# Delta rule in a hybrid decoder step: 16x16 diagonal blocks of the inverse on VectorE, query-key products after it, and a seventh buffer for q, k, v and z

## The chip, the cores and the metric

The kernel runs on one core of one Trainium2 chip. TensorE (PE) multiplies matrices and loads its weights through a row of its own (PEld); VectorE (DVE), ScalarE (ACT) and GpSimd (POOL) work element by element; SyncE (SP) starts most of the DMAs. The metric is the device time of one execution in microseconds (us), lower is better. Several runs are given by their median. The trace is that of one profiled execution; times in it count from its first instruction.

## The reference

One inference step of a decoder with two layers, for a prompt of 256 tokens and for 8 samples of one token each, all in fp32. A layer has a mixer (four mLSTM heads and eight gated-delta heads behind one input projection `w_in`), cross attention over 256 memory tokens, and a SwiGLU. The change lies in the gated-delta heads of the prompt. Cut to these:

```python
def gdn_chunked(q, k, v, log_a, beta, S0):
    incl, strict = lower triangle with and without the diagonal
    def step(S, xs):                                   # one chunk of the sequence
        g = jnp.cumsum(gc, axis=1)
        decay_ts = jnp.exp(jnp.where(incl, g_t - g_s, -jnp.inf))
        A = jnp.where(strict, decay_ts * (k k^T) * beta, 0.0)
        rhs = vc - exp(g) * (kc @ S)
        U = triangular_solve(A, rhs, lower=True, unit_diagonal=True)
        wu = beta * U
        qk = (qc kc^T) * decay_ts
        o = exp(g) * (qc @ S) + qk @ wu
        S_new = exp(g_last) * S + (wend * kc)^T @ wu
        return S_new, o
```

What matters: per chunk and head a unit lower triangular system is solved, (I + A) U = rhs, and the products of q and k are needed only for the output `o`, after U is known.

## The kernel before

**Streams.** Nearly all matmul work is weights times activations. `stream` (L249) multiplies 2048 rows of a weight matrix by 264 columns (256 tokens and 8 samples). Weights arrive in blocks of 512 KB (`block`, L239): a DMA from SP brings `raw`, ACT copies it rounded as `wh`, DVE takes `wl` = `raw` - `wh`, and PE adds three products for each piece (high times high, high times low, low times high). `wh` and `wl` have three buffers each. ACT and DVE do this with raised priority.

**The order on PE.** PE's instructions are written out in the order in which the program issues them; the other engines' orders are made by the framework's planner, from priorities (program order, raised in some places) and its own estimates of when an operation can start. Small work that isn't a stream (decay, delta rule, samples, norms) is written as generators. `yield 2100.0` means: go on when the program's own clock, which counts estimated nanoseconds of PE work (`mm`, L67), is that much further. After each piece of a stream `pump` (L89) continues whatever is due. `finish` (L96) continues generators until given ones have ended, without streams between.

**The mixer stage** (`mixers`, L1091) goes through four pairs of delta heads. For each pair three streams make q, k and v, with a causal convolution of four taps on DVE (`gdn_inputs`, L831); from the second pair on a fourth stream makes z of the pair before (`gdn_z`, L852). q, k, v, z and the mLSTM's q, k and z come from one tag of buffers, "s", with `SB` = 6 of them (L553). After a pair's streams `gdn_prompt` (L594) is started for the 256 tokens, as two chunks of 128 for each of two heads, four matrices of 128x128 side by side (index i), and `gdn_sample` (L757) for the samples. A pair's `gdn_prompt` waits until that of the pair before has set `formed` (L738).

**`gdn_prompt`**, in the order of its visits to PE:

- transposes of k (`pkn`), then the products k k^T (`pk_`) and k q^T (`pq_`), four each, and on DVE the matrices N (k k^T scaled by the decay E and by beta) and W (k q^T times E) (L621 to L629);
- after 4500 of the clock the transposes of v (DVE makes `vn`), after 1600 those of q;
- the inverse begins: `Dm` starts as four identities; the level b = 1 is done on DVE with a mask `up[1]` (`u`, L648 to L651); `Dt` holds the transposes of Dm's 32x32 blocks;
- after 2700 the transposes of N (`pa`, copied by ACT to `A`, L653 to L656);
- the levels b = 2, 4, 8, 16, 32, 64 (L657 to L694) double the inverted diagonal blocks. Each has two visits: after 2100 the products `pp` of A and Dm, which DVE copies with a mask to `f`; after 1900 the products `pd` of Dt and f, which DVE subtracts from Dm. Up to b = 16 DVE then transposes Dm into Dt again;
- for each of the two chunks (L698 to L737): `pu` (inverse times right side), then `pS` (the new state, and W times the solution for the output), with the products `pr` of q and k with the state between the chunks.

At the end the outputs are normalised, and once z is there transposed (`oT`, L749), multiplied by z and split for the output projection. `finish(*gd[:4])` and `finish(*gd[4:])` (L1146, L1151) stand in front of the projection's two parts for these heads.

`copy` (L53) is ScalarE, `tt` and `stt` (L56, L59) are VectorE unless another engine is given. Rows of the profile carry these helpers' lines: L72 is `mm`, L76 `tr`, L54 `copy`, L57 `stt`, L60 `tt`.

Of the kernel before, what the change touches and what calls it, by code (L numbers as in the profile page):

```python
# [8 lines left out]
F32 = mybir.dt.float32  # L9
F32R = mybir.dt.float32r  # L10
AF = mybir.ActivationFunctionType
ALU = mybir.AluOpType
AX = mybir.AxisListType
PSUM = bass.MemoryType.PSUM

P = 128
D = 2048
# [9 lines left out]
XH = 4  # L27
MEM = 256
EPS = 1e-6
WB, VB, SB, NV = 10, 6, 6, 6  # L30
PRIO = 1000
Q0, K0, V0, O0 = 0, 512, 1024, 2048
IF0 = 3072
# [5 lines left out]
def bc(ap, axis, n):  # L39

    a = ap.unsqueeze(axis)
    shape = list(a.shape)
    shape[axis] = n
    return a.to_broadcast(shape)
# [3 lines left out]
def kernel(ctx: ExitStack, tc: tile.TileContext, io: dict, outs: list):  # L48
    nc = tc.nc
    (y_p, y_s, p_C, p_n, p_m, p_S, p_conv, p_k, p_v, s_C, s_n, s_m, s_S, s_conv) = outs  # L50
    act, dve, pool, pe = nc.scalar, nc.vector, nc.gpsimd, nc.tensor

    def copy(out, in_, scale=1.0):  # L53
        act.activation(out, in_, AF.Copy, scale=scale)  # L54

    def stt(out, a, s, b, o0, o1):  # L56
        dve.scalar_tensor_tensor(out=out, in0=a, scalar=s, in1=b, op0=o0, op1=o1)  # L57

    def tt(out, a, b, op, eng=None):  # L59
        (eng or dve).tensor_tensor(out=out, in0=a, in1=b, op=op)  # L60
# [6 lines left out]
    def mm(out, lhsT, rhs, start=True, stop=True):  # L67
        n = 1
        for x in rhs.shape[1:]:
            n *= x  # L70
        clock[0] += max(n, lhsT.shape[-1]) / 2.4 * (1 if rhs.dtype == F32R else 4)
        pe.matmul(out=out, lhsT=lhsT, rhs=rhs, start=start, stop=stop)  # L72
# [29 lines left out]
    cp = ctx.enter_context(tc.tile_pool(name="const", bufs=1))  # L102
# [7 lines left out]
    def ps(name):  # L110
        return pm.tile([P, 512], F32, name=name, tag="m")


    ident = cp.tile([P, P], F32, name="ident")
# [10 lines left out]
    def power(t, e):  # L125

        if len(t.shape) == 3:
            e = e[:t.shape[0], :t.shape[1] * t.shape[2]].rearrange("p (a b) -> p a b", a=t.shape[1])
        else:
            e = e[:t.shape[0], :t.shape[1]]  # L130
        tt(t, t, e, ALU.pow, pool)
# [7 lines left out]
                       channel_multiplier=1)  # L139

    up = {}
    b = 1
    while b < P:
        nb = P // (2 * b)
        m = cp.tile([P, nb], F32, name=f"up{b}")
        dve.memset(m, 1.0)
        pool.affine_select(out=m, in_=m, pattern=[[-2 * b, nb]], compare_op=ALU.is_ge, fill=0.0, base=0,
                           channel_multiplier=1)
        pool.affine_select(out=m, in_=m, pattern=[[2 * b, nb]], compare_op=ALU.is_ge, fill=0.0, base=b - 1,
                           channel_multiplier=-1)  # L150
        up[b] = m
        b *= 2

    twos = cp.tile([P, GH + MH], F32R, name="twos")
    dve.memset(twos.bitcast(F32), 0.0)
# [412 lines left out]
    def four(t):  # L568
        return t.rearrange("p (i t) -> p i t", i=4)

    def hc(t):
        return t.rearrange("p (h c) t -> p h c t", c=2)


    def gdn_decay(g, G, M, R):
# [15 lines left out]
        yield 2400.0  # L591
        R.E, R.eL = E, eL

    def gdn_prompt(l, g, s, G, M, R):  # L594
        h0 = 2 * g
        q, k, v = s

        def ch(t, i):
            return t[:, i // 2, (i % 2) * P:(i % 2 + 1) * P]
# [4 lines left out]
        E, eL = R.E, R.eL  # L604
# [13 lines left out]
        dve.tensor_scalar(out=kd, in0=kss, scalar1=0.25, scalar2=None, op0=ALU.mult)  # L618
        power(kd, hp)

        pk_, pq_ = ps("kk"), ps("kq")  # L621
        for i in range(4):
            mm(pk_[:, i * P:(i + 1) * P], ch(k, i), ch(k, i))
        for i in range(4):
            mm(pq_[:, i * P:(i + 1) * P], ch(k, i), ch(q, i))
        N, W = M.w("N"), M.w("W")
        for i in range(4):
            stt(N[:, i], pk_[:, i * P:(i + 1) * P], bs[:, i:i + 1], E[:, i], ALU.mult, ALU.mult)
        tt(W, four(pq_), E, ALU.mult)  # L629
        yield 4500.0  # L630
        pv = ps("vT")
        for i in range(4):
# [9 lines left out]
            act.activation(M.junk()[:, :P], pqn[:, i * P:(i + 1) * P], AF.Square, accum_out=qd[:, i:i + 1])  # L642
        dve.tensor_scalar(out=qd, in0=qd, scalar1=4.0 * EPS, scalar2=float(DK), op0=ALU.add, op1=ALU.mult)
        power(qd, hm)

        Dm, Dt, A = M.w("Dm"), M.w("Dt"), M.w("A")
        pool.tensor_copy(out=Dm, in_=bc(ident, 1, 4))
        u = M.v("u", (4, 64))  # L648
        tt(u, N[:, :, 1::2], bc(up[1], 1, 4), ALU.mult)
        tt(Dm[:, :, 1::2], Dm[:, :, 1::2], u, ALU.subtract)  # L650
        dve.transpose(Dt.rearrange("p i t -> p (i t)"), Dm.rearrange("p i t -> p (i t)"))  # L651
        yield 2700.0
        pa = ps("NT")  # L653
        for i in range(4):
            tr(pa[:, i * P:(i + 1) * P], N[:, i])
        copy(A, four(pa))  # L656
        b = 2  # L657
        while b < P:
            def halves(t, which, i=None):
                x = t.rearrange("p i t -> p (i t)") if i is None else t[:, i]  # L660
# [32 lines left out]
                dve.transpose(Dt[32:64, :, 0:32], Dm[0:32, :, 32:64])  # L693
            b *= 2  # L694

        o = M.w("o")
        S1 = None
        for c in range(2):  # L698
            yield 1600.0
            if c == 0:  # L700
                rhs = hc(vn)[:, :, 0]
            else:
                pr = ps("pr")
                for j in range(2):
                    mm(pr[:, j * P:(j + 1) * P], ch(k, 2 * j + 1), S1[:, j])
                for j in range(2):
                    mm(pr[:, T + j * P:T + (j + 1) * P], ch(q, 2 * j + 1), S1[:, j])
                rhs, qS = M.v("rhs"), M.v("qS")
                for j in range(2):
                    stt(rhs[:, j], pr[:, j * P:(j + 1) * P], G.en[:, h0 + j:h0 + j + 1], vn[:, 2 * j + 1], ALU.mult,  # L710
                        ALU.add)
                for j in range(2):
                    copy(qS[:, j], pr[:, T + j * P:T + (j + 1) * P], scale=G.eg[:, h0 + j:h0 + j + 1])
                yield 1800.0
            pu = ps("pu")
            for j in range(2):
                mm(pu[:, j * P:(j + 1) * P], Dm[:, 2 * j + c], rhs[:, j])
            w = M.v("wu")
            tt(w, pu[:, :T].rearrange("p (h t) -> p h t", h=2),
               bc(bs.rearrange("p (h c) -> p h c", c=2)[:, :, c], 2, P), ALU.mult)  # L720
            yield 1800.0
            pS_ = ps("pS")
            for j in range(2):
                mm(pS_[:, j * P:(j + 1) * P], kw[:, 2 * j + c], w[:, j])
            for j in range(2):
                mm(pS_[:, T + j * P:T + (j + 1) * P], W[:, 2 * j + c], w[:, j])
            Sn = M.v("S")
            po = pS_[:, T:].rearrange("p (h t) -> p h t", h=2)
            if c == 0:
                copy(Sn, pS_[:, :T].rearrange("p (h t) -> p h t", h=2))  # L730
                copy(hc(o)[:, :, 0], po)
            else:
                for j in range(2):
                    stt(Sn[:, j], S1[:, j], eL[:, j:j + 1], pS_[:, j * P:(j + 1) * P], ALU.mult, ALU.add)
                nc.sync.dma_start(out=p_S[l, 0, h0:h0 + 2].rearrange("h k v -> k h v"), in_=Sn)
                tt(hc(o)[:, :, 1], po, qS, ALU.add)
            S1 = Sn  # L737
# [14 lines left out]
        x = M.w("ox", (2, T))  # L752
# [338 lines left out]
    def mixers(l, nx, mx, st, nx2):  # L1091
# [26 lines left out]
        for g in range(4):  # L1118
            if g % 2 == 0:
                hs[g // 2] = hidden(f"gd{g}")  # L1120
            r = Run()
            r.z, r.E, r.at = None, None, 2 * (g % 2)
            r.formed, r.before = False, R[g - 1] if g else None
            r.hh, r.hl = hs[g // 2]
            R.append(r)
            S = st.tile([P, 2, NB, P], F32, name="S", tag="st")
            for j in range(2):
                nc.gpsimd.dma_start(out=S[:, j], in_=io["state_gdn_S"][l, :, 2 * g + j].rearrange("b k v -> k b v"))
            spawn(gdn_decay(g, G, M, r))
            if g == 0:  # L1130
                s = gdn_inputs(l, g, nx, cb, rawc, M, first)
            else:
                s = gdn_inputs(l, g, nx, cb, rawc, M)
            gd.append(spawn(gdn_prompt(l, g, s, G, M, r)))
            gd.append(spawn(gdn_sample(l, g, s, G, M, r, S, smp)))
            if g:
                gdn_z(l, g - 1, nx, M, R[g - 1])
# [315 lines left out]
    with tc.manual_schedule(engines={mybir.EngineType.PE}):  # L1453
# [25 lines left out]
        for c in range(3):  # L1479
            w = P if c < 2 else NB  # L1480
            mm(pr[:w, c:c + 1], nx.sa[0][:, c * P:c * P + w], ones[:, 0:1])
        for c in range(3):
            w = P if c < 2 else NB
# [3 lines left out]
        for q in range(4):  # L1487
            qs = slice(q * 512, (q + 1) * 512)
            for c in range(3):
                w = P if c < 2 else NB  # L1490
                o = nx.y[:w, c, qs]
                i = nx.pt[c][:w] if q == 3 else o
# [37 lines left out]
```

## Time and profile before

| what | value |
|---|---|
| median of 3 runs | 2990.75 us (2990.35 to 2992.3) |
| profiled execution | 2992.1 us, its span 2990.2 us |
| mean granted clock of PE | 0.997 |
| PE / DVE / ACT / POOL busy | 2929.9 / 2004.4 / 1466.8 / 496.4 us |
| instructions | 58126 |

The page gives busy times by engine, the span in 40 slices of 74.75 us with a digit for the tenths that each engine is busy, the chain of work that ended last, and groups of instructions by line, engine and operation. Other views give busy times in chosen windows, and the single instructions in order of time. Matmuls overlap in PE's pipeline, so their single durations add up to more than PE's busy time, which counts the time in which at least one is under way.

### The profile page before, as it was taken

The numbers are of one execution on the slowest core, as the hardware profiler recorded it, in microseconds if no ns is written. First come the engines' busy times: TensorE is split into PE (matmuls) and PEld (weight loads), VectorE is DVE, ScalarE is ACT, GpSimd is POOL, SyncE is SP. The second block draws the span as 40 slices with busy tenths as digits, with TensorE's granted clock in tenths as the row PEclk, the third lists the DMA queues.
The fourth block names the chain that finished last, engine by engine and source line by source line (L and its number), as shares of the span: only waits on it lengthen the run. The fifth ranks groups of instructions, "written<-read, shape, count | busy, mean of one in ns | idle before, by whom it ended". The sixth has DMA issues, their size and how long they took to land.

```text
span 2990.2 us, 58126 instructions
## 1 busy us (share of the span) xinstructions
PE 2929.9 (98%) x23475; PEld 2852.7 (95%) x23475; DVE 2004.4 (67%) x3365; ACT 1466.8 (49%) x2441; POOL 496.4 (17%) x660
## 2 busy tenths in 40 slices
PE   8999999999999999999999999999999999999998
PEld 7999999978999999999999999999699999999998
DVE  7888776877555555555688777678765555555555
ACT  6555455666433333333465555556564333334335
POOL 5222100352100000000231121003520000000001
PEclk9999999999999999999999999999999999999999
DMA  7555565666666666666655554756756666666664
GB/s 198 144 149 153 154 205 165 215 211 189 182 180 181 182 179 183 178 182 180 176 156 162 145 162 131 221 157 212 232 171 183 178 182 181 180 182 179 182 180 132
DMA packets 381251, 530.09 MB, mean 177 GB/s; under 512 B 25576, under 2 KB 226224, under 8 KB 380960
## 3 DMA queue, kind: packets, MB, share of 16 engines
q1 hardware_dynamic: 364328, 498.74, 56.2%
q0 software_dynamic: 7424, 25.20, 2.8%
q10 hardware_dynamic: 9232, 2.45, 0.4%
q8 instruction: 184, 3.01, 0.4%
q14 instruction: 83, 0.68, 0.1%
HBM read 502.88 MB, written 23.83 MB: 176 GB/s over the span
## 4 chain that ended last, share of the span: by engine, by line
PE 85%; DVE 8%; ACT 3%; issue 2%; DMA 1%; POOL 0%; SPq 0%; POOLq 0%; DVEq 0%; ACTq 0%
PE acc L72 75%; DVE wl L60 2%; PE kv L72 2%; DVE xl L57 1%; PE pd L72 1%; PE pp L72 1%; ACT wh L54 1%; DVE y L57 1%; DMA memn<-in_mem_prompt_dram 1%; PE dks L72 1%; PE sqC L72 0%; PE dS L72 0%; DVE xT L60 0%; PE accg L72 0%; DVE p L1325 0%
## 5 line engine op out<-in xcount | busy, mean ns | idle before, releaser
L60 DVE TENSOR_TENSOR wl<-raw,wh 128x1024 fp32r<-128x1024 f32 x880 | 1090.8, 1240 | 797.7 <-ACT wh L54 795.9
L54 ACT ACTIVATE wh<-raw 128x1024 fp32r<-128x1024 f32 x880 | 931.1, 1058 | 1242.2 <-PE acc L72 1130.1
L72 PE MATMUL acc<-xh,wh 128*128 128x264 f32 x4736 | 1367.6, 289 | 5.7 <-ACT wh L54 3.4
L72 PE MATMUL acc<-xh,wl 128*128 128x264 f32 x4736 | 1348.7, 285 | 0.9 <-DVE wl L60 0.7
L72 PE MATMUL acc<-xl,wh 128*128 128x264 f32 x4736 | 1347.5, 285 | 1.7 <-DVE xl L57 1.7
L72 PEld LDWEIGHTS acc<-xh,wh 128*128 128x128 f32 x4736 | 894.6, 189 | 10.5 <-issue 3.6
L72 PEld LDWEIGHTS acc<-xl,wh 128*128 128x128 f32 x4736 | 895.6, 189 | 4.7 <-DVE xl L57 2.3
L72 PEld LDWEIGHTS acc<-xh,wl 128*128 128x128 f32 x4736 | 893.9, 189 | 2.3 <-DVE wl L60 2.3
L72 PE MATMUL acc<-ffh,wh 128*128 128x264 f32 x1408 | 400.8, 285 | 0.6 <-DVE xT L60 0.5
L72 PE MATMUL acc<-ffl,wh 128*128 128x264 f32 x1408 | 400.8, 285 | 0.0
L72 PE MATMUL acc<-ffh,wl 128*128 128x264 f32 x1408 | 400.3, 284 | 0.0
L60 POOL TENSOR_TENSOR fg<-fg,rstd 128x264 f32<-128x264 f32 x88 | 95.3, 1112 | 1306.0 <-ACT fg L1412 1306.0
L72 PEld LDWEIGHTS acc<-ffh,wh 128*128 128x128 f32 x1408 | 264.8, 188 | 1.0 <-issue 1.0
L72 PEld LDWEIGHTS acc<-ffl,wh 128*128 128x128 f32 x1408 | 265.3, 188 | 0.0
L72 PEld LDWEIGHTS acc<-ffh,wl 128*128 128x128 f32 x1408 | 265.0, 188 | 0.0
L60 DVE TENSOR_TENSOR xT<-acc,xT 128x264 f32<-128x264 f32 x512 | 190.5, 422 | 18.9 <-PE acc L72 18.6
L60 POOL TENSOR_TENSOR sa<-sa,sq 128x264 f32<-128x264 f32 x96 | 94.4, 1001 | 177.7 <-ACT sq L313 177.4
L57 DVE SCALAR_TENSOR_TENSOR xl<-xT,cst,xh 128x264 fp32r<-128x264 f32 x96 | 78.3, 851 | 0.6 <-ACT xh L54 0.5
L54 ACT ACTIVATE wm<-r,msk 72x128 fp32r<-72x128 f32 (+1 forms) x192 | 69.0, 427 | 17.0 <-PE dS L72 14.2
L57 DVE SCALAR_TENSOR_TENSOR y<-y,cst,y 128x255 f32<-128x255 f32 (+1 forms) x144 | 63.0, 476 | 0.5
L54 ACT ACTIVATE xh<-xT,cst 128x264 fp32r<-128x264 f32 x80 | 39.6, 506 | 29.0 <-DVE xT L60 29.0
L60 POOL TENSOR_TENSOR vl<-vc,vh 128x512 fp32r<-128x512 f32 x32 | 44.5, 1418 | 26.5 <-ACT vh L54 24.3
(510 smaller groups left out, 3360.8 us busy)
## 6 DMA issues: line engine op xcount, KB each, us to landing
raw<-in_w_in_dram SPq DMA_DIRECT2D x224, 512.0 KB
raw<-in_ffn_w_gate_dram SPq DMA_DIRECT2D x176, 512.0 KB
raw<-in_ffn_w_up_dram SPq DMA_DIRECT2D x176, 512.0 KB
raw<-in_ffn_w_down_dram SPq DMA_DIRECT2D x176, 512.0 KB
raw<-in_w_out_dram SPq DMA_DIRECT2D x64, 512.0 KB
S<-in_state_gdn_S_dram POOLq DMA_DIRECT2D x16, 512.0 KB, 6.8
out_dram<-S SPq DMA_DIRECT2D x16, 512.0 KB
Ct<-in_state_mlstm_C_dram POOLq DMA_DIRECT2D x8, 1024.0 KB, 7.7
```

Of the source, the lines that this page charges most:

```text
L54: act.activation(out, in_, AF.Copy, scale=scale)
L57: dve.scalar_tensor_tensor(out=out, in0=a, scalar=s, in1=b, op0=o0, op1=o1)
L60: (eng or dve).tensor_tensor(out=out, in0=a, in1=b, op=op)
L72: pe.matmul(out=out, lhsT=lhsT, rhs=rhs, start=start, stop=stop)
```

## The change

The constant `BASE` = 16 is new, and `SB` goes from 6 to 7. The masks `up[b]` are made from b = 16 on. A small constant `eye` holds, for each of 128 partitions, the row of a 32x32 identity.

A new function `base_blocks` inverts the 16x16 diagonal blocks of I + N by substitution on DVE. ACT copies the 32x32 diagonal blocks of the four matrices to `Nc` (128 partitions, 8 blocks of 16 columns). `D` starts as identity (POOL). In five rounds of three columns DVE transposes columns of Nc, each repeated 16 times, which puts row k of a block beside all its partitions; for each k from 15 down to 1 it multiplies column k of D by this row and subtracts the product from D's first k columns. At the end D is transposed in 32x32 blocks, copied by ACT to the diagonal of `Dm`, which POOL has set to zero, and Dm is transposed to `Dt`.

In `gdn_prompt` `base_blocks` is called right after N. The level b = 1 and the levels 2, 4, 8 go; the loop starts at b = 16. Between the transposes of N and the loop stands `yield 20000.0`. The products of k and q and the matrix W move from the first visit to behind the loop; the `yield 1600.0` of the first chunk moves in front of them, so that they share its visit with `pu`.

```diff
-WB, VB, SB, NV = 10, 6, 6, 6
+WB, VB, SB, NV = 10, 6, 7, 6
+BASE = 16
...
-    b = 1
+    b = BASE
     while b < P:
         nb = P // (2 * b)
...
+    eye = cp.tile([P, 32], F32, name="eye")
+    dve.tensor_reduce(out=eye, in_=ident.rearrange("p (n x) -> p x n", x=32), axis=AX.X, op=ALU.add)
...
+    def base_blocks(N, Dm, Dt, u):
+        Nc, D = u[:, 0], u[:, 1].rearrange("p (x i) -> p x i", i=BASE)
+        N3, room = Nc.rearrange("p (i t) -> p i t", i=4), Dt.rearrange("p i t -> p (i t)")
+        for r in range(0, P, 32):
+            copy(N3[r:r + 32], N[r:r + 32, :, r:r + 32])
+        pool.tensor_copy(out=u[:, 1].rearrange("p (a t) -> p a t", a=4), in_=bc(eye, 1, 4))
+        tmp = room[:, 3 * P:].rearrange("p (x i) -> p x i", i=BASE)
+        for k0 in range(BASE - 1, 0, -3):
+            ks = range(max(1, k0 - 2), k0 + 1)
+            w = len(ks)
+            src = Nc.rearrange("p (x k) -> p k x", k=BASE)[:, ks[0]:ks[0] + w]
+            dve.transpose(room[:, :w * P], bc(src, 3, BASE))
+            R = room[:, :w * P].rearrange("p (k x i) -> p k x i", k=w, i=BASE)
+            for k in reversed(ks):
+                tt(tmp[:, :, :k], bc(D[:, :, k], 2, k), R[:, k - ks[0], :, :k], ALU.mult)
+                tt(D[:, :, :k], D[:, :, :k], tmp[:, :, :k], ALU.subtract)
+        dve.transpose(Nc, u[:, 1])
+        for r in range(0, P, 32):
+            copy(Dm[r:r + 32, :, r:r + 32], N3[r:r + 32])
+        dve.transpose(room, Dm.rearrange("p i t -> p (i t)"))
...
-        pk_, pq_ = ps("kk"), ps("kq")
+        pk_ = ps("kk")
...
-        for i in range(4):
-            mm(pq_[:, i * P:(i + 1) * P], ch(k, i), ch(q, i))
-        N, W = M.w("N"), M.w("W")
+        N = M.w("N")
...
-        tt(W, four(pq_), E, ALU.mult)
+        Dm, Dt = M.w("Dm"), M.w("Dt")
+        pool.memset(Dm, 0.0)
+        base_blocks(N, Dm, Dt, M.v("u", (2, P)))
         yield 4500.0
...
-        Dm, Dt, A = M.w("Dm"), M.w("Dt"), M.w("A")
-        pool.tensor_copy(out=Dm, in_=bc(ident, 1, 4))
-        u = M.v("u", (4, 64))
-        tt(u, N[:, :, 1::2], bc(up[1], 1, 4), ALU.mult)
-        tt(Dm[:, :, 1::2], Dm[:, :, 1::2], u, ALU.subtract)
-        dve.transpose(Dt.rearrange("p i t -> p (i t)"), Dm.rearrange("p i t -> p (i t)"))
+        A = M.w("A")
         yield 2700.0
...
         copy(A, four(pa))
-        b = 2
+        yield 20000.0
+        b = BASE
         while b < P:
...
+        yield 1600.0
+        pq_ = ps("kq")
+        for i in range(4):
+            mm(pq_[:, i * P:(i + 1) * P], ch(k, i), ch(q, i))
+        W = M.w("W")
+        tt(W, four(pq_), E, ALU.mult)
         o = M.w("o")
         S1 = None
         for c in range(2):
-            yield 1600.0
             if c == 0:
                 rhs = hc(vn)[:, :, 0]
             else:
+                yield 1600.0
                 pr = ps("pr")
```

## The prediction, made before the changed kernel was built or run

> **What bounds the kernel now.** I read the page from the top, then went into the stage that the change touches.
>
> ```profile
> PE 2929.9 (98%) x23475; PEld 2852.7 (95%) x23475; DVE 2004.4 (67%) x3365; ACT 1466.8 (49%) x2441; POOL 496.4 (17%) x660
> DVE  7888776877555555555688777678765555555555
> ...
> PE 85%; DVE 8%; ACT 3%; issue 2%; DMA 1%; POOL 0%; SPq 0%; POOLq 0%; DVEq 0%; ACTq 0%
> ```
>
> TensorE (PE) is busy for 2929.9 of 2990.2 us, and the chain that ended last runs through it for 85%. VectorE (DVE) is at 67% overall, but the slices say where it is tight: 6 to 8 tenths in the first ten of the 40 slices and again in the ten from slice 21, which hold the two mixer stages, where the delta rule runs. The view by windows cuts these stages out: first the delta rule of layer 0 and of layer 1, then, inside them, the stretch of each of the eight head pairs from the end of its matrix N to its first matmul for blocks of 16. The columns are the window, its length, and the busy time of PE, PEld, DVE, ACT and POOL, then clock and DMA.
>
> ```profile
> 85.00:387.00 302.00, 296.08 (x2534) 288.03 (x2533) 241.80 (x560) 168.25 (x408) 61.16 (x107) 1.00 0.51 148
> 1545.00:1870.00 325.00, 317.06 (x2687) 307.88 (x2686) 259.10 (x591) 178.65 (x434) 65.32 (x115) 0.99 0.51 148
> 104.90:131.50 26.60, 24.28 (x200) 23.90 (x200) 25.39 (x57) 13.77 (x32) 7.50 (x15) 1.00 0.67 193
> 177.20:207.90 30.70, 30.70 (x261) 30.34 (x259) 25.05 (x45) 12.75 (x24) 5.28 (x12) 1.00 0.52 151
> 251.10:281.90 30.80, 30.80 (x262) 30.44 (x261) 24.14 (x45) 14.99 (x35) 6.41 (x16) 1.00 0.47 137
> 324.30:352.20 27.90, 27.90 (x228) 27.57 (x227) 20.37 (x41) 11.92 (x25) 3.95 (x9) 1.00 0.43 127
> 1559.80:1591.70 31.90, 31.82 (x262) 31.43 (x263) 30.25 (x76) 22.16 (x58) 7.02 (x15) 1.00 0.48 137
> 1643.30:1673.60 30.30, 28.79 (x231) 28.58 (x231) 23.32 (x42) 11.73 (x22) 5.98 (x13) 0.96 0.57 163
> 1722.20:1750.30 28.10, 28.10 (x238) 28.10 (x238) 24.24 (x43) 12.98 (x25) 5.26 (x13) 1.00 0.62 188
> 1795.90:1826.20 30.30, 30.30 (x248) 29.97 (x247) 22.27 (x44) 12.87 (x26) 5.15 (x10) 1.00 0.48 141
> ```
>
> PE idles 302.00 - 296.08 = 5.9 us in the first stage and 7.9 us in the second: what PE doesn't have to do there is time gained, as long as nothing else becomes late. DVE has room of 1.2, 5.7, 6.7, 7.5, 1.7, 7.0, 3.9 and 8.0 us in the eight stretches. These are the two sides of this change: it takes work from PE and gives work to DVE exactly there.
>
> **What leaves PE.** The levels b = 2, 4, 8 go: each has one visit of four `pp` products and one of four `pd` products, for 8 head pairs, so 3 x 2 x 8 = 48 visits. The timeline of PE shows one visit between the weight streams, and the groups of instructions show all of them:
>
> ```profile
> 124.51 0.29 PE L72 MATMUL acc<-xh,wl 128*128 128x264 f32 x1
> 124.64 1.00 PE L72 MATMUL pp<-Dm,A 128*128 128x64 f32 x8
> 125.45 0.37 PE L72 MATMUL acc<-xh,wh 128*128 128x264 f32 x1
> 125.65 0.28 PE L72 MATMUL acc<-xl,wh 128*128 128x264 f32 x1
> 125.77 0.28 PE L72 MATMUL acc<-xh,wl 128*128 128x264 f32 x1
> ...
> L72 PE MATMUL pd<-Pf,Dt 128*128 128x64 f32 x256 | 32.4, 269 | 0.1
> L72 PE MATMUL pp<-Dm,A 128*128 128x64 f32 x256 | 32.3, 269 | 3.8 <-DVE y L57 2.3 <-ACT A L54 1.5
> ```
>
> A matmul of fp32 stands twice in the trace (four are x8), and matmuls are pipelined, so durations can't be added; starts can. Stream matmuls follow each other by 0.12 us. From 124.51 to 125.77 are three more of them, which alone would take 0.36; the visit therefore costs 1.26 - 0.36 = 0.90 us. 48 x 0.90 = **43.2 us** leave PE. The 256 records of each group fit: 4 levels (2, 4, 8, 16) x 4 x 2 x 8.
>
> The idle time of 3.8 us stands before the first `pp` of a pair, which comes about 2 us after the transposes of N and waits for their copy `A`. In the new order 20 us of PE's own clock lie between, so it goes: **-3.8 us**.
>
> The query-key products are moved, not removed: eight records per pair, before in the visit of `kk`, now in the visit of `pu`, so no visit is added; I cost them at nothing. Their product W (one DVE operation) now lies between `pu` and `pS`. It starts while `pu` runs and delays `wu` by less than its own length; the 1.8 us of streams in front of `pS` hide it, and without that cover 8 such operations would be some 5 us.
>
> **What DVE gets.** The rows, by operation and form:
>
> ```profile
> L691 DVE STREAM_TRANSPOSE Dt<-Dm 128x512 f32<-128x512 f32 x32 | 22.6, 705 | 0.5
> L60 DVE TENSOR_TENSOR Pf<-pp,up 128x256 f32<-128x256 f32 x32 | 13.3, 416 | 6.3 <-PE pp L72 5.7
> L60 DVE TENSOR_TENSOR Dm<-Dm,pd 128x256 f32<-128x256 f32 x32 | 13.3, 414 | 17.2 <-PE pd L72 16.8
> L60 DVE TENSOR_TENSOR dx<-db,sz 128x16 f32<-128x16 f32 x8 | 1.3, 167 | 0.1
> L693 DVE STREAM_TRANSPOSE Dt<-Dm 32x128 f32<-32x128 f32 x8 | 2.4, 300 | 0.2
> L60 DVE TENSOR_TENSOR wl<-raw,wh 128x1024 fp32r<-128x1024 f32 x880 | 1090.8, 1240 | 797.7 <-ACT wh L54 795.9
> L54 ACT ACTIVATE g_t<-pc 32x264 f32<-32x264 f32 x2 | 0.8, 384 | 0.0
> ...
> 98.41 0.34 DVE L798 TENSOR_SCALAR dqn<-dks,der 8x128 f32<-8x128 f32 x1
> 98.77 0.34 DVE L57 SCALAR_TENSOR_TENSOR dvn<-dks,da,dvn 8x128 f32<-8x128 f32 x1
> ```
>
> Removed per pair: four rounds (the level b = 1 has no `Pf` but the mask product `u` of the same size) of 0.416 + 0.414 + 0.705 = 1.54, so **6.1 us**. Added: for k = 15 down to 1 two operations of 8k elements. Between 16 and 256 elements the rows give (416 - 167)/240 = 1.04 ns an element on 150 ns; the sum of 8k is 960, so 2 x (15 x 150 + 960 x 1.04) ns = 4.5 + 2.0 = 6.5 us. Each depends on the one before; such a pair in the timeline starts 0.36 us apart at a length of 0.34, so 30 x 0.02 = 0.6 us more. Five transposes of 384 elements, between 300 and 705, are 0.57 each, 2.9 us; the two at the end are 0.30 and 0.71. Together **11.0 us**, 4.9 us more than before. The Trainium skill, "VectorE: DVE Perf Modes", section "Rules for kernel authors", speaks against this edit: it says that chained operations should be made few, whatever is saved in their size. The trace agrees: in the 167 ns of the smallest row only 17 are elements.
>
> No row has these operations with such short inner rows and repeated elements; the bounds are the 150 ns floor alone for each of the 30 (2 us less per pair) and the 128x256 row for each (6 us more). I take the line between the rows. ACT gets eight copies of 32x128 per pair, at most the 0.384 of 32x264, 3 us; ACT is busy for 168 of 302 us and hides them as load, but half of them stand in front of the chain and half behind it. POOL gets a memset and a small copy for one large copy, and eight masks fewer at the start; hidden, 0 to 1 us.
>
> **The wait that can come.** The result must be there when PE reaches its first matmul for b = 16. Before, 12 us of planned yields and six visits lay between the transposes of N and that point; now 20 us of yields and none, so the eight stretches keep their length and the chain from pair to pair its pace. The stretch must hold 4.9 us more of chain work, 0.7 less because W leaves, and, since PE does streams instead of 6 x 0.9 = 5.4 us of visits, two more weight blocks, 2 x 1.24 = 2.5: 6.7 us more. Against the rooms above, the excess is 5.5, 1.0, 0, 0, 5.0, 0, 2.8, 0 us: 14.3 in all. What can go behind are the convolution taps:
>
> ```profile
> L57 DVE SCALAR_TENSOR_TENSOR y<-y,cst,y 128x255 f32<-128x255 f32 (+2 forms) x12 | 5.2, 471 | 0.0
> L57 DVE SCALAR_TENSOR_TENSOR S<-S,gs,dS 128x128 f32<-128x128 f32 x16 | 4.4, 330 | 0.0
> ...
> 1642.43 1.08 PE L76 MATMUL qT<-ident,s 128*128 128x128 f32 x4 [1.98 <-DVE S L57]
> 1643.16 0.57 PE L72 MATMUL acc<-xh,wh 128*128 128x264 f32 x1
> 1643.53 0.42 PE L72 MATMUL acc<-xl,wh 128*128 128x264 f32 x1
> 1643.75 0.42 PE L72 MATMUL acc<-xh,wl 128*128 128x264 f32 x1
> ```
>
> The first two rows are groups of DVE in the first stretch. 5.2 us of taps could wait, and then nothing is late; but the 4.4 us of updates of S in the first pair of each layer can't, since their PSUM buffers are wanted again, and the lines from PE's timeline show what happens then: PE stands for 1.98 us until DVE has read one. Afterwards the stream's starts lie 0.22 us apart instead of 0.12 for some 2.5 us, about 1.2 us more (12 matmuls x 0.10). The Trainium skill, "TensorE: Matmul & The Clock Gate", section "What's actually happening", puts the fall to half clock at an idle window of about 3.4 us; by it a wait of 2 us costs itself only. The trace doesn't agree: 1.98 us were enough here.
>
> With no taps put behind, 14.3 us of waits and three falls of the clock at 1.2 are 17.9; with all of them behind, 0. I take **13 us**, nearer to the upper end, since the copies on ACT lengthen the chain and the first pairs have no room. If instead DVE's present idle time couldn't be used at all (it is short waits for ACT and PE), it would be 8 x 6.7 + 8 x 1.2 = 63.
>
> The seventh buffer lets z, q and k of later pairs be written while a pair still holds its own; the streams now run 5.4 us further ahead per pair. I cost it at nothing. Without it the next q would wait for the products `pr` of an earlier pair. At the end of the stage there is slack:
>
> ```profile
> 402.97 0.38 PE L76 MATMUL oT<-ident,o 128*128 128x128 f32 x2
> ...
> 483.55 0.28 PE L72 MATMUL acc<-gd2h,wh 128*128 128x264 f32 x1
> ```
>
> The last pair is done at 403, and its product is first read by a stream at 483.6; 21.6 us less of PE before that leaves over 50.
>
> **Sum.** -43.2 - 3.8 + 13 = **-34 us**. The profiled execution took 2992.1 us (span 2990.2), so it becomes 2958; the median of the runs shown is 2990.75, 1.3 lower, so **2957 us**.
>
> **The rivals.**
> - *Everything is hidden* (waits 0 to 3 us): 2943 to 2947. For it: the taps alone are as large as the worst excess. Against it: the first pairs. 0.18.
> - *The forecast*, waits of 4 to 23 us: 2948 to 2968. 0.47.
> - *DVE is late in most pairs*, waits of 24 to 41 us: 2968 to 2985. For it: short dependent operations leave gaps that DVE's order may fill with taps, and the chain then takes as long as all the work in the stretch. 0.18.
> - *DVE becomes the bound, slower than before*: the chain of the 16x16 blocks ends late in all eight pairs because idle time in the stretches can't be used; 63 us of waits, -47 + 63 = +16, about 3007. It decides from 47/8 = 5.9 us of wait per pair, the clock's share among it. Against it: only two stretches have less than 3 us of room. 0.08.
> - *It doesn't do what it says*: the freed matmuls aren't on the path, because weights or their splitting set the pace; then only the 3.8 us go, 2987. Against it the feed-forward stage, where PE is never idle at a faster flow of weights (735.00 busy of 735 us). With waits of 41 to 53 us, which end in the same place, 0.09.
>
> ```profile
> 740.00:1475.00 735.00, 735.00 (x6037) 735.00 (x6037) 410.84 (x546) 293.92 (x320) 49.99 (x52) 1.00 0.61 181
> ```
>
> **How the numbers follow.** Differences under about 0.2%, 6 us, can't be told from no change. Faster by more: 0.18 + 0.47 + 0.18 = 0.83; the same: 0.09; slower: 0.08. The range from 2943 to 2985 holds the first three cases and leaves out 0.17 above, and a little below if a visit costs more than 0.90.
>
> **What would show it.** `pp` and `pd` with 128x64 fall from 256 to 64 records each. DVE's busy time rises by about 40 us, and a stretch between N and the first `pp` is over 95% busy. PE's waits before `pp` name DVE's `Dm` or `Dt`; those of `qT`, `dS` or `NT` name `S` or `vn`. The two delta-rule stages are each some 17 us shorter and every later stage as long as before. I am wrong if a link of the chain costs over 0.3 us, if the clock falls in every pair, or if the stages shrink by the full 43 us.

## The result, and the profile after

| | before | after |
|---|---|---|
| median | 2990.55 us (2989.83 to 2992.3, 4 runs) | 3008.92 us (3007.0 to 3012.34, 4 runs) |
| ratio | | 1.0064, 95% interval 1.0051 to 1.0076 |
| profiled execution | 2992.1 us, span 2990.2 | 3007.11 us, span 3005.4 |
| mean granted clock of PE | 0.997 | 0.988 |

The changed kernel is 18 us slower, where 34 us less had been forecast. Single runs in a second, slower state (4892 and 3365 us, in two of the kernels below) are left out of the medians here. First the page after: busy times, DVE's slices, the chain that ended last.

```profile
PE 2908.8 (97%) x23091; PEld 2831.1 (94%) x23091; DVE 2022.4 (67%) x3562; ACT 1486.4 (49%) x2505; POOL 503.2 (17%) x660
...
DVE  7888776877555555555688877778775555555555
...
PE 74%; DVE 6%; ACT 3%; issue 2%; DMA 1%; POOL 1%; POOLq 0%; ACTq 0%; DVEq 0%
```

PE has 384 matmul records fewer, and yet its share of the last chain falls from 85% to 74%: more of the end is set by what PE waits for. The two windows that hold nearly all of the two delta-rule stages say how much. In the view by windows the columns are window and length, busy time of PE, PEld, DVE, ACT and POOL, the granted clock, and the DMAs (their busy share and GB/s). Before:

```profile
85.00:425.00 340.00, 334.08 (x2842) 325.81 (x2841) 272.73 (x614) 189.88 (x446) 62.85 (x109) 1.00 0.53 153
1550.00:1900.00 350.00, 342.87 (x2897) 333.76 (x2896) 277.79 (x621) 191.28 (x448) 63.52 (x111) 1.00 0.52 152
```

and after:

```profile
85.00:425.00 340.00, 312.74 (x2554) 302.62 (x2554) 274.44 (x696) 189.55 (x459) 63.22 (x111) 0.96 0.50 145
1550.00:1900.00 350.00, 323.52 (x2640) 313.66 (x2639) 282.25 (x714) 196.00 (x471) 71.65 (x117) 0.96 0.51 146
```

PE's idle time in them goes from 5.9 + 7.1 = 13.1 to 27.3 + 26.5 = 53.7 us, 40.7 more; the 3.8 us that left the first `pp` are already inside this difference. The clock falls from 1.00 to 0.96. Part of the time at half clock lies in the waits themselves and costs nothing: after, 46.7 us of busy PE ran at half clock, which is 23.4 us lost, and before 3.4 us, which is 1.7. Together with the 43.2 us of products that were to leave PE: -43.2 + 40.7 + 21.7 = +19, and 18.4 were measured. PE's part of the sum therefore holds, and the waits ate it. The view of PE's waits (what it waited for; us in total, times, longest) names them:

```profile
PE pp L73 <- ACT Dm L55: 22.9, 5, 6.4
PE dS L73 <- ACT wm L55: 10.9, 5, 3.9
...
PE dks L77 <- POOL kv L792: 4.9, 2, 2.6
...
PE sqC L73 <- DVE sl L61: 3.3, 2, 1.7
PE dks L77 <- POOL mvn L926: 3.2, 2, 2.4
...
PE pp L73 <- issue: 1.7, 1, 1.7
```

`Dm` is ACT's copy of the finished 16x16 blocks, so `pp` waits for the end of DVE's chain. The one wait without a cause is of the same kind: `pp` starts at 1611.79, and ACT's last copy into `Dm` ends at 1611.68. So `pp` waits for 24.6 us, in six of the eight pairs. `dS`, `dks` and `sqC` belong to the samples and to the mLSTM heads; nothing of them was changed.

How long does the chain take? It has 37 operations per pair on DVE, called links here, each of which waits for the one before, for its result or for the room that it used. They are as short as forecast. Groups of DVE after, the five transposes per pair, the large transpose at the end, and the longest and the shortest of the 30 products and differences:

```profile
L611 DVE STREAM_TRANSPOSE Dt<-u 128x384 f32<-128x384 f32 x40 | 22.8, 571 | 3.6 <-ACT u L55 3.6
L619 DVE STREAM_TRANSPOSE Dt<-Dm 128x512 f32<-128x512 f32 x8 | 5.6, 705 | 6.8 <-ACT Dm L55 6.8
...
L61 DVE TENSOR_TENSOR u<-u,Dt 128x120 f32<-128x120 f32 x8 | 2.2, 275 | 0.0
...
L61 DVE TENSOR_TENSOR u<-u,Dt 128x8 f32<-128x8 f32 x8 | 1.3, 166 | 0.1
```

The 37 links of a pair add up to 10.5 us; 11.0 were forecast. But from the start of the first to the end of the last they take 36.2, 33.0, 32.6, 39.0, 41.4, 34.3, 34.3 and 31.8 us in the eight pairs. The timeline of DVE in the second pair shows why (start, length, operation):

```profile
190.73 0.58 DVE L611 STREAM_TRANSPOSE Dt<-u 128x384 f32<-128x384 f32 x1
191.23 0.65 DVE L61 TENSOR_TENSOR vn<-vT,kd 128x512 f32<-128x512 f32 x1
191.81 0.27 DVE L61 TENSOR_TENSOR Dt<-u,Dt 128x120 f32<-128x120 f32 x1
191.99 0.76 DVE L61 TENSOR_TENSOR y<-acc,rstd 128x264 f32<-128x264 f32 x2
192.68 0.27 DVE L61 TENSOR_TENSOR u<-u,Dt 128x120 f32<-128x120 f32 x1
192.86 1.23 DVE L61 TENSOR_TENSOR wl<-raw,wh 128x1024 fp32r<-128x1024 f32 x1
194.01 0.27 DVE L61 TENSOR_TENSOR Dt<-u,Dt 128x112 f32<-128x112 f32 x1
...
194.60 0.68 DVE L61 TENSOR_TENSOR ox<-oT,sz 128x512 f32<-128x512 f32 x1
...
207.82 0.20 DVE L61 TENSOR_TENSOR u<-u,Dt 128x40 f32<-128x40 f32 x1
210.22 0.16 DVE L812 TENSOR_SCALAR dqk<-dqk 8x4 f32<-8x4 f32 x1 [2.20 <-ACT junk L811]
210.30 0.17 DVE L61 TENSOR_TENSOR Dt<-u,Dt 128x32 f32<-128x32 f32 x1
...
223.00 0.71 DVE L619 STREAM_TRANSPOSE Dt<-Dm 128x512 f32<-128x512 f32 x1 [0.85 <-ACT Dm L55]
```

Between two links stand splittings of weights (`wl`), taps (`y`) and outputs of the pair before (`ox`); and at 207.82 the next link, whose data is ready, stands for 2.2 us behind a sample's `dqk` that waits for ACT. From 190.73 to 223.71 are 33.0 us for 37 links: 0.9 us a link. Over the eight pairs it is 0.9 to 1.1 us.

And what a late `Dm` costs on PE, from its timeline:

```profile
223.02 1.97 PE L73 MATMUL pp<-Dm,A 128*128 128x64 f32 x8 [3.78 <-ACT Dm L55]
...
225.12 0.42 PE L73 MATMUL acc<-xl,wh 128*128 128x264 f32 x1
225.34 0.42 PE L73 MATMUL acc<-xh,wl 128*128 128x264 f32 x1
```

PE stands for 3.78 us; then `pp` takes 1.97 instead of 1.00 us and the stream goes at 0.22 us a matmul instead of 0.12.

### The profile page after: what moved, and what is told of

The parts are those of the page before. It is cut to its first block, busy times and chain, and to the rows that moved or that the text cites. A ratio compares the mean times of both kernels' runs of the same rounds, so it can differ in the third digit from the quotient of the medians.

```text
span 3005.4 us, 57593 instructions
## 1 busy us (share of the span) xinstructions
PE 2908.8 (97%) x23091; PEld 2831.1 (94%) x23091; DVE 2022.4 (67%) x3562; ACT 1486.4 (49%) x2505; POOL 503.2 (17%) x660
## 4 chain that ended last, share of the span: by engine, by line
PE 74%; DVE 6%; ACT 3%; issue 2%; DMA 1%; POOL 1%; POOLq 0%; ACTq 0%; DVEq 0%
PE acc L73 68%; DVE wl L61 2%; DVE xl L58 1%; PE kv L73 1%; DMA memn<-in_mem_prompt_dram 1%; ACT wh L55 1%; DVE xT L61 0%; PE sqC L73 0%; PE dS L73 0%; PE pp L73 0%; PE dks L73 0%; DVE p L1355 0%; POOL sa L61 0%; PE pd L73 0%; DVE y L58 0%
## 5 line engine op out<-in xcount | busy, mean ns | idle before, releaser
L61 POOL TENSOR_TENSOR vl<-vc,vh 128x512 fp32r<-128x512 f32 x32 | 44.7, 1417 | 24.1 <-ACT vh L55 21.7
```

## The experiments

Two theories run through the expectations. **A**: the loss is PE's wait for the end of the chain, which other work between the links stretches. **B**: VectorE has no room left in these stages; whatever is put first, something else comes late. Every run stands beside runs of the kernel before on the same chip (medians 2989.5 to 2992.4 us); ratios are to those, with their 95% intervals.

**Is PE's saving real?** The substitution is left out, the rest of the change stays.

```diff
-        pool.memset(Dm, 0.0)
-        base_blocks(N, Dm, Dt, M.v("u", (2, P)))
+        pool.tensor_copy(out=Dm, in_=bc(ident, 1, 4))
+        dve.transpose(Dt.rearrange("p i t -> p (i t)"), Dm.rearrange("p i t -> p (i t)"))
```

> Leaves out the substitution: Dm starts as identity, so only the levels from 16 on are computed; PE's order is that of the changed kernel. This is the gain on PE by itself. If my term for PE was right (48 visits of 0.90 us and 3.8 us of waits), the time is 2943 to 2952 us and the matmul 'pp' waits for nothing. If what was freed on PE isn't on the path, or the moved products, the longer yield or the seventh buffer cost time by themselves, it is 2965 us or more.

2946.7 us, 0.9857 [0.9843, 0.9872]. No wait at `pp` is left, and the 43 us that the forecast took from PE are there. All of the loss, 3008.9 - 2946.7 = 62 us, hangs on the substitution. In the two windows PE idles for 13.4 us without it and for 53.7 with it: 40 of the 62 us are idle time, and the other 22 are the clock.

**Does priority shorten the chain?**

```diff
-        base_blocks(N, Dm, Dt, M.v("u", (2, P)))
+        with tc.high_priority(offset=PRIO):
+            base_blocks(N, Dm, Dt, M.v("u", (2, P)))
```

> The changed kernel with the whole substitution at raised priority, so that the planner doesn't put taps and sample work between its links; same work. Theory A (the order on VectorE makes a chain of some 11 us last 32 us, and PE waits for it): the waits before 'pp' fall from 22.9 us to under 5, time 2955 to 2985 us. Theory B (VectorE is full in these stretches; it doesn't matter what comes first): waits of the same sum appear before other matmuls (dS, dks, sqC, acc), time 2997 us or more.

3005.54 us, 1.0053 [1.0036, 1.007]; chains of 28.6 to 39.7 us, and `pp` still waits for 18 us. DVE's order hardly moves: in the second pair its 83 operations from the first link on stand in the same order as without the priority. So this run doesn't test what a chain without work between its links would do. That the planner doesn't put a link earlier that it expects later is likely, but not shown.

**The moved products alone**, in the kernel before:

```diff
-        for i in range(4):
-            mm(pq_[:, i * P:(i + 1) * P], ch(k, i), ch(q, i))
...
+        yield 1600.0
+        pq_ = ps("kq")
+        for i in range(4):
+            mm(pq_[:, i * P:(i + 1) * P], ch(k, i), ch(q, i))
+        W = M.w("W")
+        tt(W, four(pq_), E, ALU.mult)
```

> The kernel before with only the query-key products and W moved behind the levels (six buffers as before, the levels 2, 4, 8 kept). I cost this at nothing: 2988 to 2993 us by both theories. Over 2996 us, the move itself would have a price, through W in front of 'pS'.

2997.83 us, 1.0028 [1.0017, 1.004]: 8 us slower. PE's waits for `dS` rise from 1.2 to 7.8 us and those for `NT` to 2.8; how the move makes samples late wasn't traced. The run without the substitution has the same move; if PE saves the 47 us of the forecast, about 4 are lost there (43 to 44 found).

**More cover for the chain**, that is, more stream work on PE before `pp`: `yield 20000.0` becomes `yield 22000.0`.

> The changed kernel with yield 22000 in place of 20000 in front of the level 16, about 2.2 us more of streams for each pair. Theory A: PE arrives 2.2 us later at a result that is ready at the same time, so the waits before 'pp' (five of up to 6.4 us, 22.9 in sum) fall to about 13 and the clock falls less often: 2990 to 3001 us. Theory B: as the changed kernel, 3005 to 3012 us, with waits elsewhere.

2995.82 us, 1.002 [1.0011, 1.003], 13 us better than the changed kernel. PE's waits there:

```profile
PE dS L73 <- ACT wm L55: 11.3, 4, 3.9
PE pp L73 <- ACT Dm L55: 9.7, 4, 3.0
...
PE pp L73 <- POOL kv L792: 3.9, 1, 3.9
```

The last of these also ends with ACT's last copy into `Dm` (copy to 1609.30, `pp` from 1609.40). So the wait for `Dm` goes from 24.6 to 13.6 us, and the one for `dS` stays. A explains the first, not the second. More than 22 us of cover wasn't tried.

**Taps behind the chain.** The taps and the gate of later streams are ordered behind the last operation of the chain that came before them in the program; then the same with 22 us.

```diff
+            with behind():
+                twice_silu(r, y)
...
+    def behind():
+        return tc.issue_after(last[-1]) if last else nullcontext()
```

> The changed kernel with the convolution taps (and the product behind them) of later streams queued on VectorE behind the last operation of the substitution of the pair that has begun; all work is kept, only VectorE's order differs. Theory A (the chain is late because other work stands between its links): the chain shortens from 32 us to about 20, the waits of 'pp' fall from 22.9 us to under 6, time 2970 to 2992 us. Theory B (VectorE is full): the taps come late instead, q, k and v with them, the waits of 'dks', 'acc' or 'kT' grow by as much, time 2997 us or more.

> As e5, with yield 22000 as in e4. Theory A: no wait is left before 'pp'; 2965 to 2990 us, and not above e5 by more than 3. Theory B: 2995 us or more.

3063.11 us, 1.024 [1.0224, 1.0255], and 3059.94 us, 1.0232 [1.0217, 1.0247]. The chains do get shorter, 15.8 to 37.5 us, five of them under 29, and `pp` waits for 3.8 us only. But PE's waits now read

```profile
PE dks L77 <- POOL kv L797: 55.6, 4, 18.2
PE dks L77 <- POOL mvn L933: 34.6, 2, 18.2
```

A late tap makes the samples' q, k and v late, and PE's written order has their products in front of the next stream. The 5.2 us of taps that the prediction wanted to put behind couldn't go there. So the samples were moved too, `yield 7500.0` of their generator to 28000, with the taps behind the chain and without:

> e5 with the samples' visit 'dks' put 28000 instead of 7500 of the planned clock after its pair's streams, so that it comes after the substitution and the taps that e5 put behind it. In e5 the waits of 'pp' had gone (3.8 us) and 'dks' waited 90 us for taps. Theory A (each wait is a due time against VectorE's order): both waits are gone, 2950 to 2980 us. Theory B (VectorE has no room left in the mixer stage whatever the order): 2995 us or more, with waits at other matmuls.

> The changed kernel with only the samples' visit put 28000 instead of 7500 later; the taps stay where the planner puts them. The samples' small operations leave the stretch, the taps don't. Theory A: the chain loses some 3 of 32 us, the waits of 'pp' fall to 10 to 18 us and those of 'dks' (8 us) go: 2985 to 3003 us. Theory B: 3000 us or more.

3005.35 us, 1.0043 [1.0027, 1.006], and 3007.04 us, 1.0056 [1.0041, 1.0071]. With both, `dks` falls to 10 us, but `pp`, `dS`, `qT` and a stream's own `acc` wait instead. With the samples later alone `dks` doesn't wait at all, and `pp`, for which A expected 10 to 18 us, waits for 8.6 us on `Dm` and for these, which end with ACT's last copy into `Dm` too:

```profile
PE pp L73 <- issue: 22.2, 3, 10.6
```

Order moves the loss about; no order tried took it away. Both times are in B's range.

**Fewer links.** `BASE = 8` leaves the level b = 8 on PE and 14 instead of 30 links on DVE, with 14 us of cover, then 16; the other two add the later samples (20 us) and the taps behind the chain.

```diff
-BASE = 16
+BASE = 8
...
-        yield 20000.0
+        yield 14000.0
```

> The changed kernel with BASE = 8: 14 links in place of 30, the level 8 is back on PE (16 visits of 0.90 us), and yield 14000, since that level's planned time comes back. PE's gain is 32 x 0.90 + 3.8 = 33 us. Theory A: the chain has half the links, so half of the work that stands between them, and is in time: 2958 to 2985 us, waits before 'pp' under 5 us. Theory B: VectorE's work is 1.5 us a pair more than before the change, so also under 2990 us; this run doesn't separate them, it asks whether half of the change is worth more than the whole.

> As e7 with 2 us more of streams in front of the level 8. If e7 still has waits before 'pp', this is faster by them; if it has none, within 5 us of e7.

> e7 (BASE = 8, yield 14000) with the samples' visit 20000 instead of 7500 later. e7 has 5 us of waits before 'pp', 5 before 'dks' and 8.5 before 'dS'. Theory A: these fall by more than half, 2962 to 2977 us. Theory B: within 4 us of e7 (2977 to 2985 us).

> e11 with the taps behind the substitution as in e5. Theory A: no wait before 'pp' or 'dks', 2958 to 2974 us. Theory B: not faster than e7, 2977 us or more.

2979.74 us, 0.9967 [0.9954, 0.9981]; 2984.23, 0.9979 [0.9969, 0.9989]; 2982.14, 0.9971 [0.996, 0.9982]; 2980.7, 0.9968 [0.9957, 0.998]. The four are alike within their intervals. The chain's own time is 5.6 us, its length 11.0 to 25.9. Two thirds of PE's saving stay (32 of 48 visits, 29 us), and 5 to 11 us of it reach the end. In the last run the chain is short, 11.3 to 16.8 us, and `pp` waits for nothing, yet no time is gained over the first, whose `pp` waits for 4.9 us: `dks` and `dS` wait for 15 us. The last two runs came out where B had them.

**Load or wait?** The same chain, on the same engines, into a tile of its own that nobody reads, and its control without the chain. Room for the tile comes from four buffers instead of six for the samples' small tiles, in both.

```diff
-        base_blocks(N, Dm, Dt, M.v("u", (2, P)))
+        pool.tensor_copy(out=Dm, in_=bc(ident, 1, 4))
+        dve.transpose(Dt.rearrange("p i t -> p (i t)"), Dm.rearrange("p i t -> p (i t)"))
+        base_blocks(N, room4, room4, M.v("u", (2, P)))
```

> Every instruction of the chain of the 16x16 blocks runs as in the changed kernel, on the same engines, but into a tile of its own that nobody reads; Dm and Dt are the identity, as in the run without the substitution, so the inverse of the diagonal blocks is left out of the output. Room for the tile comes from four buffers instead of six for the samples' small tiles. Theory A (what costs is that TensorE waits for the end of the chain): no wait at pp, 2945 to 2960 us, like the run without the substitution. Theory B (VectorE has no room in the stage, so the load of the chain makes other results late even if nobody waits for its own): waits at dS, dks and sqC stay at 15 us or more, the clock still falls, 2975 to 2995 us. Between 2960 and 2975 both have a share, to be read from the waits.

> The control for the run beside it: no substitution, Dm and Dt the identity (the inverse of the diagonal blocks is left out of the output), and four buffers for the samples' small tiles. Both theories: 2943 to 2951 us, as with six buffers (2946.7). If it is longer by more than 6 us, the four buffers cost that, and the run beside it is to be compared with this one.

2973.38 us, 0.9941 [0.9925, 0.9958], and 2948.19 us, 0.9852 [0.9837, 0.9867]. The control says that the fewer buffers cost nothing. The load alone costs 25 us, and awaiting its result 3008.9 - 2973.4 = 36 more: **both theories have a share**, A the larger one. The chain that nobody reads is as long as the other, 27.1 to 45.5 us; VectorE has one transpose of 0.70 us per pair more there than in the changed kernel, so the load's share is rather too large than too small. The two windows with the load,

```profile
85.00:425.00 340.00, 319.23 (x2653) 309.73 (x2653) 285.54 (x718) 197.97 (x477) 60.96 (x114) 0.97 0.53 154
1550.00:1900.00 350.00, 339.16 (x2839) 330.17 (x2838) 299.53 (x747) 210.52 (x495) 68.67 (x115) 0.99 0.57 166
```

and without it,

```profile
85.00:425.00 340.00, 331.72 (x2789) 322.53 (x2788) 264.52 (x591) 197.45 (x461) 64.09 (x109) 0.99 0.57 169
1550.00:1900.00 350.00, 344.46 (x2910) 336.33 (x2908) 269.73 (x586) 199.29 (x439) 63.12 (x113) 1.00 0.60 175
```

give the same split: PE idles 31.6 against 13.8 us, and the clock takes 0.03 x 319 + 0.01 x 339 = 13 against 3. That is 28 us for the load (25 measured); from there to the changed kernel 22 us of idle time and 12 of clock, 34 (36 measured). The waits with the load, and nobody waiting for it:

```profile
PE dS L73 <- ACT wm L55: 9.7, 4, 4.2
PE sqC L73 <- DVE sl L61: 7.3, 1, 7.3
...
PE dks L77 <- POOL kv L794: 4.2, 2, 3.0
```

are the ones of samples and mLSTM in the changed kernel: B's share.

**The chain off VectorE.** The 30 (or 14) products and differences go to GpSimd; the transposes stay.

```diff
-                tt(tmp[:, :, :k], bc(D[:, :, k], 2, k), R[:, k - ks[0], :, :k], ALU.mult)
-                tt(D[:, :, :k], D[:, :, :k], tmp[:, :, :k], ALU.subtract)
+                tt(tmp[:, :, :k], bc(D[:, :, k], 2, k), R[:, k - ks[0], :, :k], ALU.mult, pool)
+                tt(D[:, :, :k], D[:, :, :k], tmp[:, :, :k], ALU.subtract, pool)
```

> The 30 products and differences of the chain run on GpSimd; the transposes stay on VectorE. From GpSimd's rows (492 ns at 128x8, 1001 ns at 128x264) an operation of 8k elements costs 0.48 us and 2 ns an element: 30 x 0.48 + 1920 x 0.002 = 18 us own time a pair, with ten changes of engine a chain of 22 to 30 us. Theory A (time goes with the end of the chain): the chain is 5 to 10 us shorter than in the changed kernel, pp waits for under 8 us in all, 2960 to 2985 us. Theory B (VectorE's load): VectorE gets about 6.5 us a pair back, waits at dS, dks and sqC fall below 12 us, 2955 to 2980 us. If GpSimd itself has no room (samples' kv and mvn, taps of its own), dks waits for POOL for over 20 us and the time stays above 3000 us.

> Blocks of 8, 14.0 us until pp, and the 14 products and differences of the chain on GpSimd: 14 x 0.48 + 896 x 0.002 = 8.5 us own time, a chain of 13 to 20 us. Theory A (only the chain's end counts, and with blocks of 8 pp waits for 5 us already): within 5 us of the run with blocks of 8 on VectorE, 2976 to 2986 us. Theory B (VectorE's load is what delays dS and dks): 2965 to 2976 us, dS and dks below 8 us together.

With blocks of 16, 2987.6 us, 0.9987 [0.9978, 0.9997]: 21 us better than the changed kernel, though just outside what either theory expected. The chains are 21.6 to 28.8 us long and `pp` waits for nothing, as A had it. `dS` waits as before, against B, and GpSimd is now late for the samples:

```profile
PE dS L73 <- ACT wm L55: 10.7, 4, 3.7
PE dks L77 <- POOL kv L792: 10.0, 4, 3.9
PE dks L77 <- POOL mvn L926: 6.4, 2, 4.0
```

With blocks of 8, **2974.42 us, 0.994 [0.9925, 0.9954], the fastest of the kernels that leave nothing out**, below both kernels compared here. Chains of 11.3 to 16.1 us; GpSimd has little to put between two links, as its timeline shows for the second pair:

```profile
193.65 0.40 POOL L61 TENSOR_TENSOR Dt<-u,Dt 128x112 f32<-128x112 f32 x1
194.13 0.44 POOL L61 TENSOR_TENSOR u<-u,Dt 128x112 f32<-128x112 f32 x1
```

It gains 5 us (8 by the ratios) on the same blocks on VectorE. The median is inside B's range, but the interval reaches into A's. By the waits the gain is A's: `pp` waits for nothing instead of 4.9 us, while `dS` and `dks` wait for 14 us together, as on VectorE (13) and not under 8. An operation is longer here than on VectorE, and the chain shorter.

**Less cover, and one buffer less**, in that kernel: `yield 14000.0` becomes 11000, with seven and with six buffers.

> As the run with blocks of 8 on GpSimd, but 11 instead of 14 us of PE's own clock until pp. The chain takes 11 to 16 us there and pp waited for nothing, so about 3 us of cover go. Theory A (the end of the chain): pp waits in the three or four pairs with the longest chains, 2 to 12 us with the clock, so 2974 to 2986 us. Theory B (room on VectorE): an earlier pp leads the chain of a pair to its end earlier and packs VectorE's work more closely; dS and dks wait as before or longer, 2972 to 2980 us. Both agree that it is no shorter than 2970 us.

> The run beside it with six instead of seven buffers for q, k, v and z: what the seventh buffer does in a changed kernel. If it does nothing, as the prediction had it: within 4 us of the run beside it. If the streams of the next pair wait for a buffer without it, ACT and DVE write q or k late, PE waits at kT or at a stream's acc, and it is 5 to 25 us longer.

2979.34 us, 0.996 [0.9946, 0.9975], and 2981.75 us, 0.9968 [0.9957, 0.998]. `pp` doesn't wait even at 11 us, against A's expectation, and 2.8 us before `NT` are new. In the two windows PE idles only 2.2 us more (22.2 against 20.0). What is lost is the clock: 0.993 against 0.996 in the profiled executions, which over 2911 us of busy PE is some 9 us; these executions are 7.8 us apart, the medians 5. The seventh buffer does nothing that can be measured. It alone, in the kernel before, wasn't tried, nor the products moved back in the changed kernel.

## Why the prediction was wrong

- **PE's saving, 43.2 us and 3.8 at the first `pp`: right.** Without the substitution the median is 2946.7 us, where 2943 to 2947 was given for waits of 0 to 3 us; in the changed kernel `pp` and `pd` with 128x64 have 64 records each, as said. Only the reading of the 3.8 us was off: their row puts 1.5 us down to the copy `A` and 2.3 to DVE's `y`, a tap.
- **The chain's own time, 11.0 us: right** (10.5).
- **The step that failed is the new wait: 13 us forecast, 62 measured** (clock included in both). It was worked out from the room in eight stretches, "14.3 in all", as if DVE were a vessel into which 6.7 us could be poured, with taps to be put behind if it overflowed. But the links wait one by one in DVE's order. The view by windows of the changed kernel, from the end of N to the first `pp`, first and fifth pair and the sum of the eight:

```profile
101.37:141.43 40.06, 33.77 (x261) 32.79 (x260) 35.52 (x94) 23.21 (x59) 8.26 (x15) 0.96 0.62 182
...
1570.78:1611.79 41.01, 35.47 (x275) 34.90 (x273) 39.07 (x111) 29.48 (x71) 12.27 (x21) 0.96 0.51 146
...
sum 294.28, PE 249.66 PEld 242.33 DVE 260.16 ACT 185.97 POOL 58.75; mean PE 31.21 PEld 30.29 DVE 32.52 ACT 23.25 POOL 7.34
```

  DVE is busy for 260 of 294 us, 88%, where over 95% was said to be the sign; only the fifth stretch reaches it, with 39.07 of 41.01 us. Room of 34 us is still there, in gaps like the 2.2 us before `dqk`, while the chain is late. "The eight stretches keep their length" was wrong too: their mean went from 29.6 to 36.8 us.
- **Two of its signs of failure were met.** One is "a link of the chain costs over 0.3 us": a product or difference costs 0.2 to 0.3 us of DVE and 0.9 us of time, since each waits in DVE's order behind work that the planner set there. The other is "the clock falls in every pair": it fell at least once in each of the eight. The Trainium skill, "VectorE: DVE Perf Modes", section "Rules for kernel authors", wants few chained operations ("Minimize op *count*, not sems"). The prediction weighed that rule by the fixed part of 150 ns only; the runs with 14 such operations instead of 30 fit it, at 2980 to 2984 against 3009 us.
- **"What can go behind are the convolution taps": wrong.** Put behind, together with the gate, they cost 54 us more, since the samples then wait; with the samples later too, next to nothing was gained (3005 us).
- **The fall of the clock, 1.2 us a wait: too small.** After the 3.78 us before `pp` the clock was 0.50 for at least 5 us (below), some 2.5 us, and in all it took 22 of the 62.
- **Moved products and seventh buffer at nothing: as far as is known right in the changed kernels** (about 4 us without the substitution, if PE saves what was forecast; 2.4 us with blocks of 8 on GpSimd, within the intervals). In the kernel before, the move cost 8 us.
- **DVE's busy time was to rise by 40 us and rose by 18.0**: links between independent neighbours overlap with them, as 191.81 + 0.27 = 192.08 against the next start at 191.99. All links together last 83.8 us and add 59.7 to DVE's busy time.
- **The stages were to be 17 us shorter each.** The first stream that reads the delta rule's product starts 12.3 us later instead (483.55 before), and its counterpart in layer 1 17.8 us later (1978.27, before 1960.52). The parts behind the two stages are 1 to 3 us shorter than they were.

```profile
495.89 0.28 PE L73 MATMUL acc<-gd2h,wh 128*128 128x264 f32 x1
```

- **The rival that came true is the fourth**, "DVE becomes the bound", about 3007 us with 63 us of waits, because idle time in the stretches can't be used. The reason given against it, that only two stretches have less than 3 us of room, counted room that can't be used. Its number is partly luck: it put everything on the chain's end in all eight pairs, while `pp` waits in six of them, and 25 us are other work made late by the load.

## What to carry to other kernels

Idle time of an engine is room for independent work, not for a chain of dependent operations: price each link at the spacing that this engine's order gives to others' operations (here 0.9 us), not at its own length. Before moving work from the busiest engine to one that is 80% busy in the same stage, look for an engine with few tenants, even if its operations are slower. To part load from latency, let the work run into a tile that nobody reads: here it split 61 us into 25 and 36.

## What was not expected of the hardware

Whether the clock falls isn't told by the length of a wait alone. Three waits of PE in the changed kernel, from its timeline:

```profile
134.19 0.44 PE L77 MATMUL dks<-ident,kv 128*128 128x128 f32 x2 [2.56 <-POOL kv L792]
...
1611.79 1.08 PE L73 MATMUL pp<-Dm,A 128*128 128x64 f32 x8 [1.66 <-issue]
...
1697.55 1.33 PE L73 MATMUL pp<-Dm,A 128*128 128x64 f32 x5 [6.40 <-ACT Dm L55]
```

and the 5 us behind three waits at `pp` (3.78, 1.66 and 6.40 us) by windows:

```profile
223.02:228.02 5.00, 5.00 (x23) 5.00 (x24) 1.81 (x3) 1.06 (x1) 0.00 (x0) 0.50 0.10 36
...
1611.79:1616.79 5.00, 5.00 (x42) 5.00 (x43) 3.46 (x7) 1.71 (x2) 1.87 (x3) 1.00 0.86 258
1697.55:1702.55 5.00, 5.00 (x22) 4.86 (x23) 2.19 (x8) 3.38 (x14) 0.69 (x1) 0.50 0.00 0
```

All seven waits of 3.7 us or more in the changed kernel's two stages were followed by half clock, at which PE then worked for 3.4 to 6.1 us. Of nine waits of 1.4 to 2.6 us three were followed by it (1.55, 1.73 and 1.90 us; also the 1.98 us in the kernel before) and six not (2.56 and 1.66 above). The ten stretches at half clock in these stages last 3.41, 6.83 or 10.24 us each, some of it during the wait. The Trainium skill, "TensorE: Matmul & The Clock Gate", section "What's actually happening", puts the fall at an idle window of about 3.4 us: for the long waits the trace agrees, and the prediction took its one short wait for the rule.
